# Hybrid decoder trunk on one core: the round of PSUM bank pairs starts each layer's first feed-forward at its third pair

## The chip, the cores and the metric

The kernel runs on one core of one Trainium2 chip. The metric is device time in microseconds. Three runs of the kernel before took 1780.59 to 1783.45 us, the median is 1781.65 us. Times called "in the trace" come from one profiled execution. Its clock starts at the first recorded instruction, so they are us from there.

## The reference, cut to what matters

`x` has 512 positions of 1024 features, float32. Two layers (DEPTH = 2), each of which does:

```python
x = x + 0.5 * swiglu(rms_norm(x, ffn1_norm[l]), ffn1_w_gate[l], ffn1_w_up[l], ffn1_w_down[l])
h = rms_norm(x, mix_norm[l])
a, g, q, k, v = split(h @ w_in[l])                  # 512 columns each
conv_out = silu(rms_norm(causal_conv31(a * sigmoid(g))))
s1, s2   = q1 @ k1.T * scale + bias, q2 @ k2.T * scale + bias     # per head, causal, QK-norm
diff_out = rms_norm((softmax(s1) - lam * softmax(s2)) @ v) * (1 - lambda_init)
x = x + concat(conv_out, diff_out) @ w_out[l]
x = x + 0.5 * swiglu(rms_norm(x, ffn2_norm[l]), ffn2_w_gate[l], ffn2_w_up[l], ffn2_w_down[l])
```

`swiglu(h, g, u, d)` is `(silu(h @ g) * (h @ u)) @ d` with 2816 hidden features. Attention has 4 heads, each with two maps over 64 features and values of 128; the convolution has 512 channels and 31 taps.

## The kernel before, in words

**Arithmetic.** `x` stays in SBUF with features on partitions. Every matrix product is done on TensorE (PE) in three float32r products: each operand is split into a high part and the rest, and `mm3` (lines 138, 141 and 142) adds high by high, rest by high and high by rest. The splits of weights are made by ACT (lines 101, 364: `whi`) and by DVE or POOL (lines 102, 368: `wlo`).

**PSUM banks.** PSUM holds 128 x 512 float32 tiles, one to a bank. `BANKS` gives two banks each to the tags "mm", "sc" and "po", one to "tp" and one to "y". A tile asks for a tag; it gets one of the tag's banks as soon as the tile that had it has been read for the last time. What asks for which:

| tag | who asks |
|---|---|
| "sc", "po", "mm" by turn | feed-forward pairs, conv inputs, K and Q projections (`pair_banks`, tile `ps_pair`), and `ps_d` by single banks |
| "sc" and "po" | scores `ps_sc` (map 0 and map 1), output products `ps_out` |
| "mm" | values `ps_v` (L892), attention outputs `ps_o` (L1018) |
| "tp" | transposes of the maps `ps_at`, sums of squares `ps_ss`, `ps_idle` at the start |
| "y" | sums and broadcasts of rows, conv sums `ps_y` and `ps_th` |

**The round.** A pair of banks is asked for by a running number, the turn:

```python
def turn_tag(turn):
    return ("sc", "po", "mm")[turn % 3]
```

A feed-forward takes 34 turns: 5 of plain gate and up products, 4 of `ps_d`, and 25 units (L378). It returns the next turn. A mixer starts with the turn that it is handed and takes 8: conv inputs 0, 1 and 2, K pair 0, K pair 1, Q pair 0, Q pair 1, conv input 3. Since 34 % 3 is 1, the layers differ before the change: layer 0's first feed-forward starts at turn 0, so its mixer starts at 34, which is "po"; both second feed-forwards start at 0; layer 1's first feed-forward therefore starts at 34, and its mixer at 68, which is "mm".

**The mixer.** Called mixer 0 and mixer 1 here, by layer. In program order: conv inputs; K and Q projections of positions in two halves each (`project`: products, then on ACT squares, on POOL the reciprocal roots at L189, on DVE the normalised `qn` at L881); transposes of `qn` back into the same two banks (`to_features`, L905), copied out by ACT as `kt` and, with two gains, as `qz` (L912). So a pair of banks of a K or Q projection is held from its first product to those copies. The last of these is `to_features(0, 1)`, the transposes of Q pair 1. Then two score steps (`attend`) alternate with four value tiles (`project_values`: L896, L897, L898 are their three products, 24 to a tile). The 31 taps of the causal convolution run beside it: channel group 0 on POOL with ACT (L943, L944), groups 1 and 2 on DVE (L958), group 3 on both, ended by the sum `u` (L963). Attention goes in 16 steps, one query block of 128 and one head each:

- scores of both maps into "sc" and "po" (L990),
- bias and row minimum on DVE (L994), exponentials on ACT (L998), the second map's in place in its bank,
- the maps combined on DVE (L1001, L1003, L1004),
- two steps later the map's transposes on PE (L1011) with ACT's copy (L1013),
- three steps later the products with the values into `ps_o` (L1020); after four heads a norm (L1029 to L1035),
- two steps after the last of the four, transposes of the result into the same bank (L1047), copied out as `acth` and `actl` (L1050).

When 8 steps have been issued, `conv_finish` (ACT L972 and L974, DVE L973, POOL L975) makes the convolution's output. Last come the output products `ps_out`: from the convolution's half first, then the attention's half for the later positions, then for the earlier.

**The order of instructions.** The list scheduler of the tile framework orders the instructions of each engine by a model of their durations; only marked instructions keep the order of the program. So which tile holds which bank also moves instructions in the orders that are built. Each engine then executes its own order and waits on semaphores.

Of the kernel before, what the change touches and what calls it, by code (L numbers as in the profile page):

```python
# [19 lines left out]
DEPTH = 2  # L20
# [48 lines left out]
def trunk(ctx: ExitStack, tc: tile.TileContext, xt, par, lamv, relb, onehot,  # L69
# [23 lines left out]
    def ring(tag, n=1024):  # L93
        dt = F32 if "raw" in tag else F32R
        return wp.tile([P, n], dt, tag=tag, name=tag, bufs=RING[tag])
# [69 lines left out]
    lead = [[ring("wraw"), ring("whi"), ring("wlo")] for _ in range(4)]  # L165
# [8 lines left out]
    lead = [[tuple(t[1:]) for t in lead[2 * m : 2 * m + 2]] for m in range(2)]  # L174
# [945 lines left out]
    pr = Prep(0, "ffn1_norm")  # L1120
# [4 lines left out]
        make_scalars()  # L1125
        make_bias()

    turn = 0
    for l in range(DEPTH):
        nxt = {}  # L1130

        def then(l2, gain):
            def after(m):
                if m == 0:
                    nxt["p"] = Prep(l2, gain)
                nxt["p"].tile(m)
            return after

        def last(m):
            nc.sync.dma_start(out[m], x[:, m, :])  # L1140

        turn = ffn(pr, gu1[l], dn1[l], then(l, "mix_norm"), turn, *((lead, aside) if l == 0 else ()))
        mixer(l, nxt["p"], then(l, "ffn2_norm"), turn)
        turn = ffn(nxt["p"], gu2[l], dn2[l], then(l + 1, "ffn1_norm") if l + 1 < DEPTH else last, 0)
        pr = nxt["p"]


# [72 lines left out]
```

## Time and profile before

| what | number |
|---|---|
| median of three runs | 1781.65 us |
| the profiled execution's own time | 1779.9 us |
| its span, first to last instruction | 1778.1 us |
| matmuls on PE | 11725, busy 1765.5 us |
| DVE, ACT, POOL busy | 1394.3, 986.9, 965.4 us |
| first output product in the trace, mixer 0 and mixer 1 | 497.16 and 1380.28 us |

How to read it: a row of a timeline has the start, the duration, the engine, the line, the operation, the tile written and the tiles read, the shapes, the count of equal neighbours put together, and in brackets the time that the engine was idle before it with what ended the idling. A row of waits has the waiting instruction, what it waited for, the sum of the waits, their count and the longest. Matmuls are pipelined, so rows of neighbouring matmuls overlap, and the distance from start to start is what one takes.

### The profile page before, as it was taken

To read this page: it belongs to the slowest core of one execution; us is meant where nothing else is said; L and a number is where in the kernel's file an instruction comes from. 1 tells how busy PE (TensorE), PEld (TensorE's weight loads), DVE (VectorE), ACT (ScalarE), POOL (GpSimd) and SP (SyncE) were. 2 spreads that over 40 slices of the span, in tenths; PEclk is the share of its full clock that TensorE was granted. 3 is DMA by queue.
4 is the path that set the end of the run, shared out by engine and by line. 5 is a ranking of instruction groups with operands and counts; after the bars stand their busy time and mean duration, and the time that the engine had idled before them with its cause. 6 is when DMAs were issued, how large, how long until landed. Compare 5 with 4: busy or idle time off the path is not lost.

```text
span 1778.1 us, 30234 instructions
## 1 busy us (share of the span) xinstructions
PE 1765.5 (99%) x11725; PEld 1617.3 (91%) x11725; DVE 1394.3 (78%) x1997; ACT 986.9 (56%) x1579; POOL 965.4 (54%) x665
## 2 busy tenths in 40 slices
PE   9999999999999999999999999999999999999999
PEld 7899999988788899999988999999877888999998
DVE  6978787868857978788767887877788588787875
ACT  6456565645844456466534664665558354564663
POOL 2276566379952156566303655653898433565661
PEclk9999999999999999999999999999999999999999
DMA  6233333423122223333332333334230232333332
GB/s 225 96 113 96 107 107 105 144 85 96 47 72 83 83 95 107 107 98 118 118 95 72 108 96 108 106 102 148 72 119 25 72 107 73 106 96 108 107 105 75
DMA packets 74225, 177.87 MB, mean 100 GB/s; under 512 B 8951, under 2 KB 30726, under 8 KB 74080
## 3 DMA queue, kind: packets, MB, share of 16 engines
q1 hardware_dynamic: 72480, 174.10, 31.1%
q8 instruction: 92, 1.51, 0.3%
q0 software_dynamic: 1312, 1.67, 0.3%
q14 instruction: 53, 0.43, 0.1%
q10 hardware_dynamic: 288, 0.16, 0.0%
HBM read 173.79 MB, written 3.42 MB: 100 GB/s over the span
## 4 chain that ended last, share of the span: by engine, by line
PE 89%; DVE 6%; issue 2%; POOL 2%; ACT 1%; DMA 0%; DVEq 0%; SPq 0%; ACTq 0%
PE ps_pair L378 48%; PE ps_pair L141 5%; PE ps_pair L142 5%; PE ps_pair L138 5%; PE ps_d L378 3%; DVE wlo L368 2%; PE ps_d L141 2%; PE ps_d L142 2%; PE ps_d L138 2%; PE ps_sc L990 2%; PE ps_pair L867 2%; PE ps_pair L868 2%; PE ps_pair L866 2%; PE ps_out L138 1%; PE ps_out L142 1%
## 5 line engine op out<-in xcount | busy, mean ns | idle before, releaser
L368 DVE TENSOR_TENSOR wlo<-wraw,whi 128x1024 fp32r<-128x1024 f32 (+4 forms) x400 | 510.3, 1277 | 171.9 <-ACT whi L364 171.4
L364 ACT ACTIVATE whi<-wraw 128x1024 fp32r<-128x1024 f32 (+4 forms) x400 | 373.6, 935 | 333.5 <-PE ps_pair L378 153.1
L355 POOL TENSOR_TENSOR wraw<-wraw 128x512 f32<-128x512 f32 (+1 forms) x100 | 127.8, 1278 | 554.7 <-DVE wlo L368 366.5
L378 PE MATMUL ps_pair<-acth,wlo 128*128 128x256 f32 x1088 | 307.9, 283 | 0.0
L378 PE MATMUL ps_pair<-actl,whi 128*128 128x256 f32 x1088 | 307.9, 283 | 0.0
L378 PE MATMUL ps_pair<-acth,whi 128*128 128x256 f32 x1088 | 307.9, 283 | 0.0
L378 PE MATMUL ps_pair<-th,whi 128*128 128x256 f32 x816 | 231.8, 284 | 1.2 <-ACT keep L427 0.4
L378 PE MATMUL ps_pair<-tl,whi 128*128 128x256 f32 x816 | 230.9, 283 | 0.0
L378 PE MATMUL ps_pair<-th,wlo 128*128 128x256 f32 x816 | 230.9, 283 | 0.0
L378 PEld LDWEIGHTS ps_pair<-actl,whi 128*128 128x128 f32 x1088 | 208.9, 192 | 0.2
L378 PEld LDWEIGHTS ps_pair<-acth,whi 128*128 128x128 f32 x1088 | 208.9, 192 | 0.2
L378 PEld LDWEIGHTS ps_pair<-acth,wlo 128*128 128x128 f32 x1088 | 208.9, 192 | 0.0
L101 ACT ACTIVATE whi<-wraw 128x1024 fp32r<-128x1024 f32 (+3 forms) x124 | 123.2, 1000 | 150.5 <-PE ps_pair L141 84.3
L141 PE MATMUL ps_pair<-actl,whi 128*128 128x512 f32 x448 | 174.6, 390 | 0.6 <-DVE actl L227 0.5
L142 PE MATMUL ps_pair<-acth,wlo 128*128 128x512 f32 x448 | 174.2, 390 | 0.0
L138 PE MATMUL ps_pair<-acth,whi 128*128 128x512 f32 x448 | 173.6, 393 | 0.1
L357 POOL TENSOR_TENSOR wraw<-wraw 128x512 f32<-128x512 f32 (+1 forms) x100 | 169.3, 1693 | 7.9
L358 POOL TENSOR_TENSOR wraw<-wraw 128x512 f32<-128x512 f32 (+1 forms) x100 | 164.3, 1643 | 7.8
L378 PEld LDWEIGHTS ps_pair<-th,whi 128*128 128x128 f32 x816 | 156.6, 192 | 3.1 <-ACT keep L427 3.1
L378 PEld LDWEIGHTS ps_pair<-th,wlo 128*128 128x128 f32 x816 | 156.6, 192 | 0.0
L378 PEld LDWEIGHTS ps_pair<-tl,whi 128*128 128x128 f32 x816 | 156.6, 192 | 0.0
L356 POOL TENSOR_TENSOR wraw<-wraw 128x512 f32<-128x512 f32 (+1 forms) x100 | 149.9, 1499 | 7.6
(203 smaller groups left out, 4402.1 us busy)
## 6 DMA issues: line engine op xcount, KB each, us to landing
wraw<-in_gu SPq DMA_DIRECT2D x172, 512.0 KB, 3.5
wraw<-in_wqkv SPq DMA_DIRECT2D x24, 512.0 KB, 3.5
wraw<-in_wag SPq DMA_DIRECT2D x16, 512.0 KB, 3.6
wraw<-in_wout SPq DMA_DIRECT2D x16, 512.0 KB, 3.5
wraw<-in_dn SPq DMA_DIRECT2D x60, 128.0 KB, 3.1
wraw<-in_dn SPq DMA_DIRECT2D x20, 384.0 KB, 3.2
wraw<-in_dn SPq DMA_DIRECT2D x28, 256.0 KB, 3.1
wraw<-in_dn SPq DMA_DIRECT2D x20, 320.0 KB, 3.5
```

What stands on the lines that cost most here:

```text
L101: S.activation(hi, raw, AF.Copy)
L138: first = T.matmul(ps, wh, xh, start=start, stop=False)
L141: T.matmul(ps, wh, xl, start=False, stop=False)
L142: T.matmul(ps, wl, xh, start=False, stop=stop)
L355: G.tensor_tensor(d, g1, u1, op=ALU.add)
L356: G.tensor_tensor(u1, u1, u2, op=ALU.add)
L357: G.tensor_tensor(m0, u1, g1, op=ALU.add)
L358: G.tensor_tensor(m1, m0, g2, op=ALU.add)
L364: pinned(S.activation(hi[:, : self.cols[k]], self.raw[k][:, : self.cols[k]], AF.Copy), pin)
L368: pinned(V.tensor_tensor(out=lo[:, :c], in0=self.raw[k][:, :c], in1=f32(hi[:, :c]), op=ALU.subtract), pin)
L378: mm = T.matmul(ps, l, r, start=first and i == n == 0, stop=False, skip_group_check=True)
L866: T.matmul(ps[n], xh[:, t], wh, start=k == 0, stop=False)
```

## The change

The turn is no longer carried from layer to layer. Each layer's first feed-forward starts at turn 2, which is "mm", and so both mixers start at turn 36, which is "sc". Second feed-forwards start at 0 as before. No instruction is added or removed.

```diff
-    turn = 0
     for l in range(DEPTH):
...
-        turn = ffn(pr, gu1[l], dn1[l], then(l, "mix_norm"), turn, *((lead, aside) if l == 0 else ()))
+        turn = ffn(pr, gu1[l], dn1[l], then(l, "mix_norm"), 2, *((lead, aside) if l == 0 else ()))
         mixer(l, nxt["p"], then(l, "ffn2_norm"), turn)
-        turn = ffn(nxt["p"], gu2[l], dn2[l], then(l + 1, "ffn1_norm") if l + 1 < DEPTH else last, 0)
+        ffn(nxt["p"], gu2[l], dn2[l], then(l + 1, "ffn1_norm") if l + 1 < DEPTH else last, 0)
```

The banks of the turns, by layer:

| | before, layer 0 | before, layer 1 | after, both layers |
|---|---|---|---|
| first feed-forward, first pair | sc | po | mm |
| conv inputs 0, 1, 2 | po, mm, sc | mm, sc, po | sc, po, mm |
| K pair 0, K pair 1 | po, mm | mm, sc | sc, po |
| Q pair 0, Q pair 1 | sc, po | po, mm | mm, sc |
| conv input 3 | mm | sc | po |
| second feed-forward, first pair | sc | sc | sc |

## The prediction

> **What bounds the kernel now.** I read the page first, then PE's waits, then the timeline around the longest wait, then stretches of the two attention stages.
>
> The page, first line and part 1:
>
> ```profile
> span 1778.1 us, 30234 instructions
> PE 1765.5 (99%) x11725; PEld 1617.3 (91%) x11725; DVE 1394.3 (78%) x1997; ACT 986.9 (56%) x1579; POOL 965.4 (54%) x665
> ```
>
> PE is busy for all but 12.6 us of the span. The change removes no matmul, so those 12.6 us, and what is hidden in matmul records whose ends are modelled, are all it can win.
>
> PE's waits over the whole execution (total, times, longest):
>
> ```profile
> PE ps_v L896 <- ACT qz L912: 1.8, 1, 1.8
> PE ps_sc L990 <- DVE e L1004: 1.4, 2, 0.7
> PE ps_o L1047 <- DVE ov L1035: 0.8, 1, 0.8
> PE ps_sc L990 <- DVE mn L994: 0.7, 2, 0.4
> ```
>
> The longest is met once although there are two mixers. Its place, in mixer 1:
>
> ```profile
> 1321.46 2.42 ACT L912 ACTIVATE qz<-ps_pair,gq 128x512 f32<-128x512 f32 x4 [1.72 <-PE ps_pair L905]
> 1324.44 1.03 PE L905 MATMUL ps_pair<-ident,qn 128*128 128x128 f32 x8
> 1325.98 1.25 ACT L912 ACTIVATE qz<-ps_pair,gq 128x512 f32<-128x512 f32 x2
> 1327.28 0.50 PE L896 MATMUL ps_v<-whi,acth 128*128 128x512 f32 x1 [1.81 <-ACT qz L912]
> ```
>
> The last Q transposes (L905, back into the banks of Q pair 1) end, ACT copies them out (L912), and only then the first value product (L896) starts: ps_v takes an "mm" bank, and here Q pair 1 has both. The same place in mixer 0, where conv_in 3 has "mm":
>
> ```profile
> 438.06 2.42 ACT L912 ACTIVATE qz<-ps_pair,gq 128x512 f32<-128x512 f32 x4 [1.72 <-PE ps_pair L905]
> 441.06 1.03 PE L905 MATMUL ps_pair<-ident,qn 128*128 128x128 f32 x8
> 442.00 0.50 PE L896 MATMUL ps_v<-whi,acth 128*128 128x512 f32 x1
> 442.34 0.40 PE L897 MATMUL ps_v<-wlo,acth 128*128 128x512 f32 x1
> 442.58 0.39 PE L898 MATMUL ps_v<-whi,actl 128*128 128x512 f32 x1
> ```
>
> There L896 follows after 0.94 us, without a gap in the records. The last two rows, 0.24 us apart, show what one product of this width takes.
>
> The attention stages by stretches (length; busy time and count of PE, PEld, DVE, ACT, POOL; granted clock; DMA share; GB/s); the last row is the end of mixer 0's second stretch:
>
> ```profile
> 441.00:469.10 28.10, 28.10 (x117) 21.19 (x116) 22.61 (x42) 23.04 (x41) 26.17 (x20) 1.00 0.13 38
> 469.10:497.20 28.10, 25.77 (x156) 19.41 (x154) 23.78 (x85) 24.37 (x69) 24.88 (x21) 1.00 0.13 38
> 497.20:520.00 22.80, 22.68 (x119) 18.88 (x117) 11.41 (x32) 9.46 (x26) 13.21 (x9) 1.00 0.29 93
> 1324.40:1352.50 28.10, 26.29 (x111) 19.61 (x110) 23.57 (x45) 21.41 (x39) 26.08 (x20) 1.00 0.12 38
> 1352.50:1380.30 27.80, 26.79 (x165) 21.47 (x163) 22.56 (x80) 24.84 (x70) 23.79 (x20) 1.00 0.12 39
> 1380.30:1415.00 34.70, 34.70 (x204) 30.52 (x205) 17.95 (x44) 12.88 (x31) 19.43 (x13) 1.00 0.30 92
> 487.00:497.20 10.20, 7.87 (x48) 5.49 (x47) 9.58 (x39) 10.06 (x31) 8.88 (x10) 1.00 0.05 21
> ```
>
> PE idles 0 + 2.33 + 0.12 = 2.45 us in mixer 0 and 1.81 + 1.01 + 0 = 2.82 us in mixer 1. Mixer 0, without the ps_v wait, idles as much, only later: from 487 to 497.2 ACT is busy for 10.06 of 10.20 us and DVE for 9.58, PE for 7.87. The chain of waits of mixer 0 says the same:
>
> ```profile
> 446.60 3.43 PE ps_sc L990 x8
> 487.09 0.49 ACT at L1013
> 494.36 0.63 ACT ps_th L972
> 495.01 0.69 DVE u L973
> 496.09 0.61 DVE ov L1035
> 496.74 0.66 PE ps_o L1047 x4
> ```
>
> From 487.09 to 496.74 it runs on ACT and DVE. So a PE wait taken out ahead of this place is partly handed back at it. That is the question here.
>
> **The change, part by part.**
>
> *Layer 0's first feed-forward starts at "mm" instead of "sc".* The built program's PE order is the same up to mixer 0's last transposes; the warm-up product L162 uses "tp", so no bank is held at the start. Cost 0; if a bank were held, one eviction, 0.7 us by L571 below.
>
> *Layer 1's first feed-forward starts at "mm" instead of "po".* Of the feed-forward before it (34 turns from "sc") the last two pairs are "mm", then "sc", so its first pairs now go to the banks used last, where before a free "po" came first. The rows there, DVE's adds into x and two products:
>
> ```profile
> 881.38 0.69 DVE L571 SCALAR_TENSOR_TENSOR x<-ps_pair,x 128x512 f32<-128x512 f32 x1
> 887.29 0.40 PE L142 MATMUL ps_pair<-acth,wlo 128*128 128x512 f32 x1
> 894.30 0.68 DVE L571 SCALAR_TENSOR_TENSOR x<-ps_pair,x 128x512 f32<-128x512 f32 x1
> 899.94 0.39 PE L141 MATMUL ps_pair<-actl,whi 128*128 128x512 f32 x1
> ```
>
> The "mm" pair is read out by 882.07 and wanted at about 887; "sc" by 894.98 and wanted at about 899.9. Both are about 5 us early: cost 0. If the cover were gone, PE would wait 894.98 − 887.29 = 7.7 us. [...]
>
> *Both mixers begin at "sc".* Then K pair 0 and 1 take "sc" and "po", Q pair 0 and 1 "mm" and "sc", conv_in 3 "po". ps_v now waits for the copies of Q pair 0: they end at 1321.46 + 2.42 = 1323.88, ahead of 1324.44, and at 440.48, ahead of 441.06. The 1.81 us of mixer 1 go, and mixer 0 loses nothing at this place.
>
> *What is late next.* Q pair 1 now has "sc", which the first scores want, so the copies L912 stand ahead of scores instead of values. The scheduler answers in the built order: 21 value products first, then the transposes, then 26 more values, and only then the first scores, where in both mixers 19 values preceded them. So first scores start 47 x 0.23 + 0.94 (the transposes, 442.00 − 441.06) = 11.7 us after the transposes' old place. In mixer 0 it was 446.60 − 441.06 = 5.5 us, in mixer 1 1327.28 + 19 x 0.23 − 1324.44 = 7.2 us: 6.2 and 4.5 us later than before. PE does not lose by that; DVE, which applies bias and minimum (L994), gets its work later. What covers it, and where the output products begin:
>
> ```profile
> 470.17 0.70 DVE L994 CUSTOM_DVE_ANT_0 ps_sc<-ps_sc,bias 128x512 f32<-128x512 f32 x1 [3.38 <-PE ps_sc L990]
> 497.16 0.50 PE L138 MATMUL ps_out<-acth,whi 128*128 128x512 f32 x1
> 1355.40 0.69 DVE L963 TENSOR_TENSOR u<-ps_y,yp 128x512 f32<-128x512 f32 x1 [3.58 <-POOL yp L944]
> 1380.28 0.50 PE L138 MATMUL ps_out<-acth,whi 128*128 128x512 f32 x1
> ```
>
> DVE has taps of the convolution to do meanwhile, and idles 3.38 and 3.58 us before it goes on. Output products begin 56.10 us after the last transposes in mixer 0 (497.16 − 441.06), 55.84 us in mixer 1.
>
> *The sum.* PE's loss I count start to start: what the distance of two matmuls exceeds the ordinary distance of their form. Over the three stretches, 392 matmuls in mixer 0 and 480 in mixer 1, the first ones the L905 rows above and the last ones these,
>
> ```profile
> 519.92 0.48 PE L142 MATMUL ps_out<-acth,wlo 128*128 128x512 f32 x1
> 1414.90 0.28 PE L141 MATMUL ps_out<-actl,whi 128*128 128x256 f32 x1
> ```
>
> that gives 5.2 and 4.35 us; the idle time of the stretches, 2.45 and 2.82, is its lower bound. For the new order, common to both mixers, I walked the engines with the durations of these rows: PE without a gap until about 48 us after the last transposes' old place, then 0.2, 0.35, about 1.0 (scores for a combined map, L1004, which costs 0.7 now), about 1.3 (values for the ps_o bank that L1050 reads), 0.25 afterwards, and 0.6 spread over many, 3.7 us in all; output products at 55.0. Bounds: 0 if nothing stalls; 5.2 if the chain of mixer 0 stays. I take 3.7, since ACT and DVE keep the same work in that stretch. At the entry of layer 0's second feed-forward a row shows one more wait, which mixer 1's order of output products, now also mixer 0's, does not have:
>
> ```profile
> 554.12 0.50 PE L141 MATMUL ps_pair<-actl,whi 128*128 128x512 f32 x1 [0.47 <-DVE actl L227]
> ```
>
> Gain: (5.2 − 3.7) + (4.35 − 3.7) + 0.47 = 2.6 us. The profiled execution took 1779.9 us, 1.75 under the median of 1781.65; so 1777.3 for such an execution, 1779.0 against the median.
>
> [...]
>
> **The rivals.**
>
> *A, the gaps go altogether.* With values done earlier, PE works ahead and ACT and DVE catch up: all idle time, 2.45 + 2.82 + 0.47 = 5.7 us, goes; 1775.9. For it: PE alone has no work to drop, and DVE's 3.4 us of idle time show slack. Against it: ACT's 10.06 of 10.20 us. Beyond it lie the whole 5.2 + 4.35 + 0.47 = 10.0 us, 1771.6, the outer bound.
>
> *B, all is given back.* The end of the convolution and ACT set the output products as in mixer 0, which has no ps_v wait and starts them 0.3 us later than mixer 1. Only the 0.47 us stay: 1781.2. For it: exactly that comparison. Against it: mixer 0 puts its idle time after a different order of scores and values.
>
> *C, slower: late scores.* If DVE's idle time is all the cover there is, 6.2 − 3.38 = 2.8 us in mixer 0 and 4.5 − 3.58 = 0.9 us in mixer 1 come on top of B: 1781.2 + 3.7 = 1784.9. With no cover it is 6.2 + 4.5 = 10.7 us, 1791.9; I price it between the two, at 1788.4. It decides once DVE has no taps left when it comes to the first scores. Against it: DVE is busy for 22.61 of 28.10 us in the stretch of the values, with work of which most does not need scores.
>
> *D, the boundary wait* of 7.7 us at layer 1's start: 1779.0 + 7.7 = 1786.7. Both 5 us margins would have to vanish.
>
> *E, the change does nothing*: the wait comes back on another tile of "mm"; 1781.65. The built order speaks against it.
>
> **How the numbers follow.** Chances: my sum 0.40 (own range 1777.0 to 1781.0, from 1 us of error in each mixer's 3.7), A 0.25, B 0.20, C 0.10, D 0.03, E 0.02. The predicted time is 1779.0. The range 1774.5 to 1784.0 reaches beyond A's 1775.9 by the part of its way to 1771.6 that I count, and up to near C's least, 1784.9; left out are D, most of C and the outer part of A, under 2 in 10. The bound of 0.2%, 3.56 us, is about what a measurement of this kernel can tell from no change: faster is under 1778.1, slower over 1785.2. Faster: A and three tenths of my sum, 0.37. Slower: D and seven tenths of C, 0.10. Same: the rest, 0.53.
>
> **What would show each step.** Right: no ps_v L896 wait on qz in PE's waits; both mixers start L896 within 0.1 us of the transposes' old place; first scores about 11.7 us after it; L138 into ps_out at about 55.0; no L571 wait at layer 1's start; the 0.47 us at L141 gone. Wrong: an idle stretch of PE ahead of the scores; new PE waits on L912, L1013 or L998 over 3.7 us in one mixer; DVE idle over 3 us before its first L994; a ps_pair wait on L571.

## The result and the profile after

The changed kernel took 1775.25 us (median of 5 runs, 1774.20 to 1777.04), the kernel before 1781.65 us. The ratio is 0.9964, 95% interval 0.9951 to 0.9978: 6.4 us or 0.36% faster. The profiled execution took 1774.20 us against 1779.9 us before.

The page of the changed kernel, first line and part 1, and PE's waits in the mixers:

```profile
span 1772.4 us, 30241 instructions
PE 1762.0 (99%) x11725; PEld 1617.0 (91%) x11725; DVE 1395.4 (79%) x1997; ACT 985.2 (56%) x1579; POOL 965.3 (54%) x665
```

```profile
PE ps_o L1020 <- DVE actl L1050: 1.7, 2, 0.8
PE ps_sc L990 <- DVE e L1004: 1.4, 4, 0.5
PE ps_sc L990 <- DVE mn L994: 0.5, 2, 0.3
```

The wait of ps_v for qz is gone. In its place stands a wait of the attention outputs (L1020) for the bank that L1050 reads, once in each mixer. The timeline of PE in mixer 0 of the changed kernel, from the last product of conv_in 3 to the first output product:

```profile
440.40 0.39 PE L142 MATMUL ps_pair<-acth,wlo 128*128 128x512 f32 x1
440.62 0.39 PE L896 MATMUL ps_v<-whi,acth 128*128 128x512 f32 x1
445.39 1.03 PE L905 MATMUL ps_pair<-ident,qn 128*128 128x128 f32 x8
452.17 1.02 PE L990 MATMUL ps_sc<-kt,qz 128*128 128x512 f32 x2
489.82 0.70 PE L990 MATMUL ps_sc<-kt,qz 128*128 128x256 f32 x2 [0.21 <-DVE e L1004]
491.43 0.49 PE L990 MATMUL ps_sc<-kt,qz 128*128 128x128 f32 x2 [0.26 <-DVE mn L994]
492.42 0.49 PE L990 MATMUL ps_sc<-kt,qz 128*128 128x128 f32 x2 [0.50 <-DVE e L1004]
493.96 1.16 PE L1020 MATMUL ps_o<-vv,at 128*128 128x128 f32 x8 [0.83 <-DVE actl L1050]
494.87 0.48 PE L138 MATMUL ps_out<-acth,whi 128*128 128x512 f32 x1
```

Values follow the last product at once; the transposes come 21 value products later, the first scores 11.55 us after the values' start. All that PE idles up to there is four waits between 489 and 494, 0.21 + 0.26 + 0.50 + 0.83 = 1.80 us. Mixer 1 repeats it to the hundredth, as the stretches of both mixers show (length; busy time and count of PE, PEld, DVE, ACT, POOL; granted clock; DMA share; GB/s):

```profile
468.70:494.90 26.20, 24.41 (x157) 19.63 (x155) 23.46 (x85) 23.28 (x72) 22.78 (x19) 1.00 0.12 41
494.90:520.00 25.10, 25.10 (x130) 21.18 (x130) 13.79 (x36) 11.37 (x29) 18.60 (x14) 1.00 0.26 86
1320.90:1349.00 28.10, 28.10 (x119) 21.29 (x119) 22.21 (x41) 22.24 (x37) 25.40 (x19) 1.00 0.12 38
1349.00:1375.20 26.20, 24.40 (x157) 19.62 (x155) 23.45 (x85) 23.28 (x72) 22.78 (x19) 1.00 0.12 41
```

**Where the time came from.** Two matmuls that stand at the same place of PE's order in both kernels bracket each mixer: the last product of conv_in 3, and a later one after which the orders agree again. Before:

```profile
440.83 0.39 PE L142 MATMUL ps_pair<-acth,wlo 128*128 128x512 f32 x1
604.50 0.39 PE L138 MATMUL ps_d<-hh,whi 128*128 128x512 f32 x1
1324.21 0.39 PE L142 MATMUL ps_pair<-acth,wlo 128*128 128x512 f32 x1
1429.30 0.28 PE L141 MATMUL ps_out<-actl,whi 128*128 128x256 f32 x1
```

After (the first of the four is the L142 row at 440.40 above):

```profile
601.00 0.39 PE L138 MATMUL ps_d<-hh,whi 128*128 128x512 f32 x1
1320.72 0.39 PE L142 MATMUL ps_pair<-acth,wlo 128*128 128x512 f32 x1
1424.21 0.28 PE L141 MATMUL ps_out<-actl,whi 128*128 128x256 f32 x1
```

| stretch | before | after | difference |
|---|---|---|---|
| start to mixer 0's bracket | 440.83 | 440.40 | −0.43 |
| mixer 0, with the entry of the second feed-forward | 163.67 | 160.60 | −3.07 |
| from there to mixer 1's bracket, the boundary between the layers in it | 719.71 | 719.72 | 0.0 |
| mixer 1 | 105.09 | 103.49 | −1.60 |
| from there to the end of the span | 348.8 | 348.2 | −0.6 |

The first and the last row do not belong to the change. The same part up to mixer 0's bracket took 440.4 to 441.6 us in the profiles below whose first feed-forwards and mixers meet as these do, whatever the banks; and the last row is one wait of 0.4 us on `keep` (L427) that the kernel before had in this execution and all but one of the other profiles lacked. So the orders of the two mixers carry 4.7 us in these two executions, and between medians some 1.7 us are left. They were looked for in the granted clock.

Only 1.7 of the 4.7 us is idle time in PE's records: the waits between the brackets add up to 2.54 us before and 1.80 after in mixer 0, and to 2.77 and 1.80 in mixer 1. The other 3 us are counted as busy, and PE's busy time on the page fell from 1765.5 to 1762.0 us. They lie in the distances from start to start around waits, many of them too short for the list. The wait of 0.47 us on `actl` that the prediction shows, at 554.12 before, has these neighbours:

```profile
553.27 0.39 PE L138 MATMUL ps_pair<-acth,whi 128*128 128x512 f32 x1
554.46 0.39 PE L142 MATMUL ps_pair<-acth,wlo 128*128 128x512 f32 x1
```

The two distances are 0.85 and 0.34 us where products of this form otherwise take 0.23 each, so this wait costs 0.73 us, not 0.47. A list of idle times leaves that part out.

### The profile page after: what moved, and what is told of

The parts are those of the page before. It is cut to its first block, busy times and chain, and to the rows that moved or that the text cites. A ratio compares the mean times of both kernels' runs of the same rounds, so it can differ in the third digit from the quotient of the medians.

```text
span 1772.4 us, 30241 instructions
## 1 busy us (share of the span) xinstructions
PE 1762.0 (99%) x11725; PEld 1617.0 (91%) x11725; DVE 1395.4 (79%) x1997; ACT 985.2 (56%) x1579; POOL 965.3 (54%) x665
## 4 chain that ended last, share of the span: by engine, by line
PE 89%; DVE 6%; issue 2%; POOL 2%; ACT 1%; DMA 0%; DVEq 0%; SPq 0%; ACTq 0%
PE ps_pair L378 48%; PE ps_pair L142 5%; PE ps_pair L141 5%; PE ps_pair L138 5%; PE ps_d L378 3%; DVE wlo L368 2%; PE ps_d L141 2%; PE ps_d L138 2%; PE ps_d L142 2%; PE ps_sc L990 2%; PE ps_pair L868 2%; PE ps_pair L867 2%; PE ps_pair L866 2%; PE ps_out L142 1%; PE ps_out L141 1%
## 5 line engine op out<-in xcount | busy, mean ns | idle before, releaser
L142 PE MATMUL ps_pair<-acth,wlo 128*128 128x512 f32 x448 | 173.9, 390 | 0.0
```

The lines of the kernel that those rows point to most:

```text
L142: T.matmul(ps, wl, xh, start=False, stop=stop)
```

## The experiments

The distance between the bracketing matmuls is the measure in each. The ratios are to runs of the kernel before on the same chip.

**Layer 0 alone.**

```diff
-        turn = ffn(pr, gu1[l], dn1[l], then(l, "mix_norm"), 2,
+        turn = ffn(pr, gu1[l], dn1[l], then(l, "mix_norm"), (2, 34)[l],
```

> Only layer 0's first feed-forward starts at the third pair (mixer 0 from "sc"); layer 1's keeps turn 34 (mixer 1 from "mm", with its wait of ps_v). Theory, that the gain comes from the whole order of mixer 0 and not from the one wait: PE's loss in mixer 0 falls from 5.2 to 3.1 us as in the changed kernel, the 0.5 us wait at the entry of layer 0's second feed-forward goes, mixer 1 keeps 4.35 us with the wait of 1.8 us: about 3 us faster than before. Rival, that the wait of ps_v is all that the change removes: mixer 0 had none, so 0. Rival, that the turn of the first feed-forward itself helps (its first matmuls start 0.4 us earlier in the changed kernel's trace): 0.4 us more than the first theory.

1777.52 us, ratio 0.9973 (0.9965 to 0.9982): 4 to 5 us faster, more than the 3 us of the theory. Mixer 0's distance is 160.61 us, as in the changed kernel. The wait of ps_v is not what was removed here, since mixer 0 never had it; this rival falls.

**Layer 1 alone**, with `(0, 2)[l]` in the same place.

> Only layer 1's first feed-forward starts at the third pair (mixer 1 from "sc"); layer 0's starts at turn 0 (mixer 0 from "po") as before. Theory, order: the loss of mixer 1 falls from 4.35 to 3.1 us, with the entry of its second feed-forward unchanged: 1.2 to 1.6 us faster. Rival, the wait goes and nothing is given back: 2.0 us faster. Rival, all the gain of 6.4 us comes from here: 6 us.

1779.77 us, ratio 0.9991 (0.9982 to 1.0000): some 1.6 us faster. Mixer 1's distance is 103.49 us, the changed kernel's, so the gain there is 1.60 us out of a wait of 1.81. But mixer 0, with the unchanged order, took 166.36 us here instead of 163.67: at the same waits its granted clock was lower, 0.97 from 469.10 to 497.20 us and 0.88 in the stretch behind:

```profile
497.20:520.00 22.80, 22.68 (x107) 18.94 (x106) 10.94 (x33) 8.62 (x24) 12.35 (x8) 0.88 0.22 71
```

Before it was 1.00 in the profile that the prediction was made from.

**Both mixers from "po"**, with `0` in the same place, and **both from "mm"**, with `1`.

> Both first feed-forwards start at turn 0, so both mixers begin at "po" as mixer 0 did before; the ps_v wait on qz is gone in both. Theory, order: mixer 1 takes over mixer 0's later waits, loss 5.2 in place of 4.35 us, and its 0.5 us at the entry of the second feed-forward: 1.4 us slower than before. Rival, the removed wait of ps_v is what counts: 1.8 us faster.

> Both first feed-forwards start at turn 1, so both mixers begin at "mm" as mixer 1 did before; the ps_v wait on qz stands in both. Theory, order: mixer 0 takes over mixer 1's loss, 4.35 in place of 5.2 us, and loses the 0.5 us wait at the second feed-forward: 1.4 us faster than before in spite of a second wait of 1.8 us. Rival, the wait of ps_v is what counts: 1.8 us slower.

"po": 1783.10 us, ratio 1.0007 (0.9998 to 1.0016), the interval reaches to no change, but it lies clearly above a gain of 1.8 us. A kernel in which the wait of ps_v is gone from both mixers is not faster than the one that has it once. "mm": 1779.20 us, ratio 0.9984 (0.9975 to 0.9993), 2.8 us faster by the ratio, with the wait in both. Both signs are those of the theory, that each starting bank has an order of its own with its own loss; the wait alone predicts the opposite ones. Part of it is the granted clock, which differs between these kernels too, so runs of equal mean clock say more: at 0.999 "po" took 1782.04 us (mean of 4) against 1781.24 of the kernel before (17 runs on the same chip), and at 1.000 "mm" took 1778.20 (5) against 1780.28 (4). The signs stay. The low clock was there again, and here it can be read product by product. Mixer 0 of the kernel with "mm" in both, around the wait:

```profile
444.29 0.50 PE L896 MATMUL ps_v<-whi,acth 128*128 128x512 f32 x1 [1.80 <-ACT qz L912]
445.11 0.40 PE L896 MATMUL ps_v<-whi,acth 128*128 128x512 f32 x1
445.34 0.40 PE L897 MATMUL ps_v<-wlo,acth 128*128 128x512 f32 x1
445.94 0.63 PE L896 MATMUL ps_v<-whi,acth 128*128 128x512 f32 x1
446.37 0.63 PE L897 MATMUL ps_v<-wlo,acth 128*128 128x512 f32 x1
446.79 0.63 PE L898 MATMUL ps_v<-whi,actl 128*128 128x512 f32 x1
448.93 0.46 PE L897 MATMUL ps_v<-wlo,acth 128*128 128x512 f32 x1
```

```profile
442.23:445.64 3.41, 1.60 (x9) 1.12 (x8) 0.93 (x3) 3.41 (x7) 3.41 (x3) 1.00 0.28 79
445.64:449.05 3.41, 3.41 (x10) 2.64 (x9) 3.27 (x5) 1.48 (x3) 3.41 (x3) 0.50 0.46 136
449.05:452.46 3.41, 3.41 (x13) 2.14 (x12) 1.35 (x4) 0.41 (x2) 2.65 (x3) 1.00 0.26 100
```

1.35 us after the wait ended (445.64 − 444.29) the distance of two products is 0.43 us instead of 0.23, for 3.41 us, with the granted clock at 0.50; in the stretch behind it the clock is 1.00. It is no wait of PE: PE counts as busy for all of the 3.41 us.

**The feed-forwards without the mixers, and the mixers without the feed-forwards.**

```diff
-        mixer(l, nxt["p"], then(l, "ffn2_norm"), turn)
+        mixer(l, nxt["p"], then(l, "ffn2_norm"), (34, 68)[l])
```

```diff
-        turn = ffn(pr, gu1[l], dn1[l], then(l, "mix_norm"), 2,
+        turn = ffn(pr, gu1[l], dn1[l], then(l, "mix_norm"), (0, 34)[l],
...
-        mixer(l, nxt["p"], then(l, "ffn2_norm"), turn)
+        mixer(l, nxt["p"], then(l, "ffn2_norm"), 36)
```

> Both first feed-forwards start at turn 2 as after the change, but the mixers are handed the turns that they had before (34 and 68, "po" and "mm"). Theory, that the mixers' order carries the gain: within 0.5 us of the kernel before, with the wait of ps_v back (1.8 us, once) and 5.2 and 4.4 us of loss in the mixers. Rival, that the bank order of the first feed-forwards or the boundary between layers carries part: faster by that part, 0.4 us if the earlier start of the first matmuls belongs to it, slower by up to 7.7 us if the boundary waits.

> The first feed-forwards start as before (turns 0 and 34), both mixers are handed turn 36 and begin at "sc". Theory: the whole gain of the change, 5.5 to 6.5 us faster than before, 3.1 us of loss in each mixer. Rival as for ffn_only: the part that belongs to the first feed-forwards is missing.

1784.07 us, ratio 1.0012 (1.0003 to 1.0020), and 1777.76 us, ratio 0.9977 (0.9967 to 0.9986). Neither is what I expected, and PE's waits say why. Each of the two has, with its own place, the same new line:

```profile
PE ps_pair L138 <- DVE x L571: 1.6, 1, 1.6
```

The edits broke the round: a feed-forward that ends on "mm" or "sc" is followed by a mixer that begins on the same tag, and its first product waits until the last pair has been added into x. That happens in layer 1 of the first kernel and in layer 0 of the second, once each, and costs 1.85 and 1.88 us of distance over the same matmuls. Allowing for it, the feed-forwards alone give about nothing, and the mixers alone about 6 us. Where no such wait stands, the distances are the known ones: mixer 1 at 105.09 ("mm") and 103.49 ("sc").

**The wait filled.** Both mixers from "mm", with work for PE in the place of its idle time:

```diff
+FILL = 16
...
                             S.activation(qz[:, m, :, t], pt, AF.Copy, scale=gq[l][:, m : m + 1])
+                if which == 0 and pair == 1:
+                    again = bank("tp", "ps_fill")
+                    for n in range(FILL):
+                        T.transpose(again[:, n % 4 * P : (n % 4 + 1) * P], qn[:, n % 4 * P : (n % 4 + 1) * P], ident)
```

> The kernel with both mixers from "mm", and behind the last transposes of each mixer 16 more transposes of the same tile into a bank that nobody reads, about 1.75 us of PE work in the place of PE's idle wait for qz. Theory, that PE's idle time of 1.8 us at this place sometimes makes the granted clock fall for the next few microseconds (seen in 2 of 5 profiles with such a wait, 0.94 over 28 to 30 us, 1.4 to 1.7 us lost): no low clock in the 30 us after this place, the slow end of the runs' spread (1781.5 with a mean clock of 0.998) goes, the median falls by 0.5 to 1.5 us from 1779.2, though PE waits as long as before. Rival, that the low clock has nothing to do with the idle time: median and spread stay at 1779.2 and 1777.7 to 1781.5, or rise by the few tenths by which the fill outlasts the wait.

The fill went where it was meant to go:

```profile
442.30 1.91 PE L917 MATMUL ps_fill<-ident,qn 128*128 128x128 f32 x16
444.28 0.50 PE L897 MATMUL ps_v<-whi,acth 128*128 128x512 f32 x1
```

The values start as late as with the wait, and the granted clock of the stretch around it (first row; second row the same stretch of the kernel without the fill) is 1.00, against 0.94:

```profile
440.00:470.00 30.00, 29.94 (x135) 23.22 (x135) 23.36 (x42) 23.24 (x41) 28.34 (x22) 1.00 0.11 36
```

```profile
440.00:470.00 30.00, 28.20 (x112) 20.92 (x111) 24.41 (x47) 21.13 (x39) 26.37 (x21) 0.94 0.11 36
```

Mean clocks of the timed runs, to three digits: 1.000 in 9 of 11 with the fill and 5 of 11 without. Averaged, 0.9998 and 0.9993; over 1780 us that is 1.0 us. The time did not follow: 1779.55 us, ratio 0.9987 (0.9978 to 0.9996), 0.3 us above the kernel without the fill. With it the scheduler also built another order of scores and maps (mixer 1 took 105.74 us at full clock instead of 105.07). The runs with a mean clock of 1.000 separate the two: 1779.44 us with the fill (mean of 9) against 1778.20 without (5), so the order lost 1.2 us, more than the clock won; the two kernels ran on different chips. So the clocks, 1.000 in 9 of 11 runs against 5 of 11, support idle time as a cause of the low clock at this place, and the forecast of a shorter median was wrong.

**The transposes pinned ahead of the values**, in the changed kernel:

```diff
-                        T.transpose(pt[:, h * P : (h + 1) * P], qn[:, h * P : (h + 1) * P], ident)
+                        tr = T.transpose(pt[:, h * P : (h + 1) * P], qn[:, h * P : (h + 1) * P], ident)
+                        if which == 0 and pair == 1:
+                            tc.keep_in_program_order(tr)
...
-                    T.matmul(ps, xh[:, t], wh, start=k == 0, stop=False)
+                    mm = T.matmul(ps, xh[:, t], wh, start=k == 0, stop=False)
+                    if j == NT - 1 and k == 0:
+                        tc.keep_in_program_order(mm)
```

> The changed kernel with the last Q transposes pinned ahead of the first value product, so that the values cannot move ahead of them; in the order built with it the first scores come after one and a half value tiles fewer gaps but the later scores wait for all eight half tiles (48 values, two scores, 48 values, two scores). Theory, that the late first scores of the changed kernel cost little because DVE has taps of the convolution meanwhile: here the second pair of score steps comes another 11 us later, beyond DVE's cover of 3.4 us, so output products begin 5 us or more later than in the changed kernel and the kernel is 3 to 7 us slower than it. Rival, that DVE's cover is larger than its idle time shows: within 1.5 us of the changed kernel.

1785.01 us, ratio 1.0016 (1.0007 to 1.0025): 9 us slower than the changed kernel, outside both expectations, and by another mechanism than I gave. The built order puts the first scores straight behind the transposes, and there PE waits for the copies of Q pair 1:

```profile
445.42 1.22 PE L994 MATMUL ps_sc<-kt,qz 128*128 128x512 f32 x1 [2.91 <-ACT qz L916]
```

```profile
440.00:470.00 30.00, 27.09 (x110) 20.34 (x109) 22.95 (x40) 20.90 (x36) 27.03 (x21) 0.94 0.12 37
1320.00:1350.00 30.00, 27.09 (x113) 20.66 (x112) 22.95 (x40) 19.87 (x34) 27.38 (x19) 0.94 0.22 70
```

It shows what the value products between transposes and scores are for here: they are the cover of the copies of Q pair 1 (L912, in this kernel L916), and without cover PE waits 2.9 us in each mixer and has a clock of 0.94 in both. It says nothing on late scores, for which it was made. But it keeps the changed kernel's round of banks and changes the order alone, and that costs 9 us, waits and clock together. No run does the reverse, new banks in an old order, so how much of the change's gain the banks would bring without the order is open.

**The changed kernel again**, and three with fewer taps of channel group 3 on POOL, `POOL_TAPS = (TAPS, 0, 0, 10)` with 8, 7 and 6 as the last number.

> The changed kernel itself, beside the next three on one chip and for a second profile. Theory, that its order has no idle time long enough to make the clock fall: granted clock 1.00 in both attention stages, the runs' mean clock 0.999 to 1.000, and the same 3.1 us of loss in each mixer; 5.5 to 6.5 us faster than before. Rival, that the first profile was lucky: a stretch with a clock of 0.93 to 0.97 as in the kernels whose mixers begin at "po".

> The changed kernel with two of POOL's ten taps of channel group 3 moved to DVE. Theory, that what is left of PE's loss in the mixers hangs on the end of the convolution on POOL and ACT, and that DVE has room while the first scores are late: POOL's sum ends 2.6 us earlier, DVE has 1.5 us more, up to 1 us less loss in each mixer, 1 to 2 us faster than the changed kernel. Rival, that DVE is the bound there: no faster, or up to 3 us slower.

> As the kernel with two taps moved, with three. Theory: within 1 us of it, if DVE's idle time of about 2.4 us ahead of the first scores covers them. Rival: slower than it by the 0.75 us of a tap in each mixer.

> As the kernel with two taps moved, with four, 3 us of DVE's time in each mixer. Theory: DVE's idle time of about 2.4 us is used up and DVE is late for the softmaxes, 0 to 2 us slower than with two taps. Rival, POOL is the bound throughout: faster still by up to 1 us.

The changed kernel: 1775.73 us, ratio 0.9964 (0.9951 to 0.9976), the same as at first. But its profile was not free of a low clock. Mixer 1 took 103.47 us, mixer 0 162.13 instead of 160.60, and its second stretch reads

```profile
470.00:500.00 30.00, 28.21 (x173) 23.50 (x172) 26.02 (x95) 26.06 (x82) 25.46 (x21) 0.94 0.11 36
```

The waits are those of the first profile, 1.8 us in all, and with them the clock was lower this time; the expectation that this idle time is too short for that falls. The two profiles are compared below, at the clock.

Taps: 1774.97, 1775.81 and 1776.65 us, ratios 0.9960 (0.9947 to 0.9972), 0.9964 (0.9952 to 0.9977), 0.9969 (0.9957 to 0.9981). Eight taps cannot be told from the changed kernel by these runs; mixer 0 took 160.80 us and mixer 1 103.71, no less than with ten. POOL's earlier end bought nothing, so the remaining loss does not hang on it alone; with six taps, where the distances grow to 161.44 and 104.33 us, PE waits 2.3 us in all for DVE's minima (L994). No version was found that is shown to beat the changed kernel.

**The distances and the clock together.** For the profiles of the kernels without fill, pinning or other taps, by the bank that the mixer begins with; "low" where a stretch of 20 to 30 us of that mixer had a granted clock under 1.00:

| begins at | mixer 0, clock 1.00 | mixer 0, low | mixer 1, clock 1.00 | mixer 1, low | low in |
|---|---|---|---|---|---|
| "po" | 163.67 | 165.05, 165.20, 166.36 | | 106.66 | 4 of 5 |
| "mm" | | 163.85 | 105.09, 105.07, 105.09 | 106.71 | 2 of 5 |
| "sc" | 160.60, 160.61, 161.07 | 162.13 | 103.49, 103.49, 103.49, 103.47 | | 1 of 8 |

A low clock added 1.4 to 2.7 us where both cases are seen. From the shares, an estimate: before, 0.8 x 1.9 (the mean of 1.4, 1.5 and 2.7) + 0.4 x 1.6 = 2.2 us; after, 2 x 0.125 x 1.5 = 0.4 us. The difference of 1.8 us is about what was left between the medians beside the 4.7 us of order. The shares rest on few profiles. The only profile of mixer 1 from "po" had a low clock, so its order has no distance at full clock.

The timed runs say the same with more cases. In three series the kernel before had a mean clock of 1.000 in 10 of 74 runs, 0.999 in 35, 0.998 in 26 and 0.997 in 3; the changed kernel, in two series, 1.000 in 6 of 10 and 0.999 in 4. At 1.000 their means are 1780.28 and 1774.95 us, 5.3 us apart; at 0.999 they are 1781.29 and 1776.47, 4.8 apart. All runs together are 6.3 us apart. So 4.7 to 5.3 us belong to the orders at an equal clock, and 1.0 to 1.8 us to how often the clock falls.

**Where the clock fell.** In the changed kernel's second profile, the stretch with the last waits of mixer 0 and the one behind it:

```profile
490.74:494.15 3.41, 1.83 (x12) 1.16 (x11) 3.41 (x14) 3.41 (x10) 3.10 (x5) 1.00 0.00 0
494.15:497.56 3.41, 3.41 (x16) 3.31 (x17) 2.14 (x11) 2.55 (x9) 3.18 (x3) 0.50 0.00 0
```

PE idles 1.58 us in the first, and the clock is 0.50 in the second. In the first profile the last three waits of mixer 0 are 0.26 + 0.50 + 0.83 = 1.59 us, and the stretches that hold and follow them have a clock of 1.00 (rows 468.70:494.90 and 494.90:520.00 above). So the same order with the same idle time had a lower clock in one execution and not in the other, and what decided between the two was not shown.

## Why the prediction was right or wrong

The time lay in the range, and the change was faster, as the likeliest case said. But the size was missed: 2.6 us forecast, 6.4 measured. Faster by over 0.2% was held less likely than no change. That the range held is in part luck: its lower end was set for rival A, whose mechanism did not come.

- *The wait of ps_v goes, mixer 0 loses nothing there.* Right: L896 starts 0.22 and 0.23 us after the last product.
- *Both feed-forward starts at no cost.* Right: 0.0 us over the boundary between the layers. The waits on L571 of the two experiments show that such a reuse does cost 1.6 us where it falls on the first product of a mixer instead of the first feed-forward. That fits the margin of about 5 us as the reason.
- *First scores 11.7 us after the transposes' old place.* 11.55 us (452.17 − 440.62). DVE waited for them, as was expected, for up to 2.7 us, in the changed kernel's waits of DVE in mixer 0:

```profile
DVE e L994 <- PE ps_sc L990: 4.3, 3, 2.7
```

  The cover held, and rival C falls for this kernel.
- *Output products at 55.0 us after that place; a loss of 3.7 us in each mixer.* This is the step that was mis-sized. They begin at 54.25 us (494.87 − 440.62, and 1375.20 − 1320.95 in mixer 1). Counted from start to start as the prediction counts, with the median distance of each form of matmul as its ordinary one, the loss over the same number of matmuls is 3.07 and 3.05 us. The four waits came to the 2.85 us forecast, though not one by one: 0.47, 0.53, 0.76 and 1.09 us for 0.2, 0.35, 1.0 and 1.3. What did not come is the rest, 0.25 afterwards and 0.6 spread over many: 0.2 us in all.
- *5.2 and 4.35 us lost before, and 0.47 at the entry.* All three are small by the same count: the mixers lost 5.40 and 4.65 us before. The 0.47 us was entered as idle time, the other terms by starts; behind the stretch mixer 0 gained 0.74 us by starts, and 0.14 us of that wait stays in the records. So the order was worth 2.33 + 0.74 + 1.60 = 4.7 us, where the prediction had 1.5 + 0.47 + 0.65 = 2.6. (The 392 and 480 matmuls count twice those that lie over the edges of two stretches; from row to row they are 387 and 476.)
- *Nothing is handed back, or everything.* Rival A's time, 1775.9 us, came close by accident, not by its mechanism: 1.80 us of idle time stay in each mixer. Rival B's argument, that ACT and DVE set the output products, is half right: what waits remain do stand at that place, on DVE.
- *No term for the granted clock.* It is 1.00 in all seven stretches of the prediction's table, which is true of that one execution and not of the kernel: in one series 29 of 33 timed runs of the kernel before had a mean clock of 0.998 or 0.999, so that it fell in most executions. The 1.75 us by which the profiled execution lay under the median were put aside as how an execution stands to its median. The lower clock is most of the other 1.7 us, by the estimates above 1.0 to 1.8 us. It goes with idle time in the runs here: 0.50 for 3.41 us behind a wait of 1.80 us in one profile of the kernel with "mm" in both, and 1.00 in the profile where transposes filled the wait.

## What to carry to other kernels

Removing the longest wait of an engine says little about the time: the mixer that had it lost less than the one that had not, and the gain went with the order that the scheduler built around the other bank. Price a wait by the starts of the matmuls around it, not by the idle time alone: 0.73 us for 0.47 here. Where the profiled execution lies at the fast end of the runs and PE idles in one place for as long as here (1.8 us), a second profile's granted clock, in stretches of a few microseconds, or the mean clock of the timed runs comes before any forecast. A round of PSUM banks that breaks at a stage boundary is worth a look at the rows: a stage that starts on the pair used last waited 1.6 us at the start of a mixer, and not at all at layer 1's first feed-forward, where about 5 us of other matmuls lie in between.

## What the runs showed of the hardware

Idle time of PE of 1.8 us, in one wait or in four within 5 us, was followed by a lower granted clock in some executions and not in others of the same order. Behind the wait of 1.80 us in mixer 0 of the kernel with "mm" in both, the clock was 0.50 for 3.41 us (distance of two products 0.43 instead of 0.23 us); behind the short waits in mixer 0 of the changed kernel's second profile it was 0.50 over 3.41 us; in mixer 0 of "Layer 1 alone" it was 0.97 over 28.1 us, in which PE idled 2.2 us, and 0.88 over the next 22.8. A low clock came in 2 of 5 mixers with the 1.8 us wait, in 1 of 8 with the four short ones, and in both mixers with 2.9 us (0.94 over 30 us in each). In mixer 1 with the wait of 1.8 us it added 1.6 us (106.71 us instead of 105.09), and those stand in no list of waits. At a clock of 1.00, mixer 1 took 103.47 to 103.49 us in four profiles of three kernels with the same order.
